# Transfers around a triangular solve moved from SyncE to GpSimd, the solve emitted later, and a norm's root moved to VectorE

## Chip, cores and metric

The kernel runs on one core of one Trainium2 chip. The metric is the device time of one execution in microseconds (us), and the median of several runs is compared. The engines are called by their names in the profile: PE (TensorE, matmuls; PEld is its weight loads), DVE (VectorE), ACT (ScalarE), POOL (GpSimd) and SP (SyncE). SP computes nothing here. It issues DMA transfers, and the row SPq shows its queue. Each engine works through its own queue in a fixed order.

## The reference

One decoder layer on 256 tokens with a model width of 2048: a norm, one input projection, two groups of heads side by side (an RWKV-7 recurrence with 16 heads of 64, and a latent attention with 8 heads), an output projection, a gated MLP with a short convolution, and a last norm. Cut to what matters here:

```python
def rwkv7_scan(r, w, k, v, a, b):
    def step(state, inp):
        r_t, w_t, k_t, v_t, a_t, b_t = inp
        sa = jnp.einsum('bhvk,bhk->bhv', state, a_t)
        state = (state * w_t[:, :, None, :]
                 + sa[..., None] * b_t[:, :, None, :]
                 + v_t[..., None] * k_t[:, :, None, :])
        return state, jnp.einsum('bhvk,bhk->bhv', state, r_t)
    ...

def rwkv7_mixer(...):
    ...
    y = rwkv7_scan(r, decay, k, v, -kk, kk * a)
    mu = jnp.mean(y, axis=-1, keepdims=True)
    var = jnp.mean(jnp.square(y - mu), axis=-1, keepdims=True)
    y = ((y - mu) * lax.rsqrt(var + GN_EPS)).reshape(bsz, s, c) * gn_w + gn_b
    bonus = jnp.sum(r * k * r_k, axis=-1, keepdims=True) * v
    return (y + bonus.reshape(bsz, s, c)) * g
```

The kernel doesn't run 256 steps. It cuts the sequence into four chunks of 64 tokens. Within a chunk the steps depend on each other through a unit triangular 64x64 matrix for each head, and the inverse of that matrix turns a chunk into a few matmuls.

## The kernel before

**Projections.** `in_tile(i)` (line 189) makes one of the 35 tiles of the input projection: 128 columns by 256 tokens, in one `mm` accumulator of PSUM. There are three such accumulators. A tile is made in two halves. For each, SP loads 512 KB of weights (`raw`, three buffers, line 127), ACT rounds them to fp32r (`hi`, line 133), DVE takes the rest (`lo`, line 134), and PE does eight matmuls with `hi` (line 163) and eight with `lo` (line 166). `hi` and `lo` have three buffers each. Tiles 17 to 24 are the value tiles, tiles 27 to 34 the latents of the attention.

**Eviction.** `shifted` (line 369) empties an accumulator: POOL clears one column of `h` (line 371), ACT copies one half of the accumulator (line 171), DVE adds the other half and scales (lines 172 and 173), ACT and DVE mix each token with the one before it (lines 374 and 375). The result is `sh`. After each pair of value tiles PE transposes them (line 612) and ACT copies them to `UV` (line 616).

**Deferred work.** `pend` holds pairs of a count and a function. `flush`, at the end of `in_tile`, calls the functions whose count is 0 and counts the others down. So a pair with count 0 is emitted after the next tile's matmuls, with count 1 after the next but one, and ahead of that tile's eviction.

**The solve and its transfers.**
- `gram` (line 511) multiplies keys and receptances of two pairs of heads on PE, and DVE masks the products into `G1` (line 529). At every second pair of tiles, 16 transfers of 16 KB (line 537, on SP) write the strict triangles of 32x32 blocks to `dL` in DRAM, two batches in all.
- `solve_load` (line 564) loads `dL` back as `Lp`, with one block per partition: 16 heads, 4 chunks and 2 diagonal blocks make 128. This is the factor.
- `solve` (line 568) inverts all the 128 blocks at once on DVE: one product with the key norms (line 575), then 31 steps of two products and sums (lines 579 and 581) on `Tq`, and a transposed copy `tp` (line 585). POOL clears `Tq` and `TT` ahead of it.
- The results go back through DRAM: `Tq` to `dT` (line 583), `tp` to `dU` (line 590), `dU` to `T11` (line 592) and `dT` to `TT` (line 596), the last two with a change of layout, all on SP.
- PE merges the blocks to 64x64 inverses (`pR`, line 625, and `pT`, line 638).

**Chunks.** `chunk(c)` (line 661) runs the recurrence: PE `px` from the state, DVE `XB`, PE `px` with `TT`, copies to `UV`, PE `pS` and `py`, DVE `ST` (the state). `group_norm(w)` (line 712) works on two chunks at a time; its root (line 723) is `rsqrt` (line 196), which is a first guess on the bits and three Newton steps. On POOL, the default, that is 14 instructions; on DVE, 11, since two steps are fused.

**Order.** A scheduler orders the instructions of each engine when the program is built, by a model of time and by the order in which the code emits them. `tc.issue_after(ins)` makes what is emitted in its block stand behind `ins` on that engine; it is an order, not a wait.

Of the kernel before, what the change touches and what calls it, by code (L numbers as in the profile page):

```python
# [9 lines left out]
F32 = mybir.dt.float32  # L10
# [4 lines left out]
ALU = mybir.AluOpType  # L15
AX = mybir.AxisListType

P = 128
# [7 lines left out]
GN_EPS = 64e-5  # L26
# [28 lines left out]
def hybrid_layer(ctx: ExitStack, tc: tile.TileContext, a: dict, out: bass.AP):  # L55
    nc = tc.nc
    V, S, PE = nc.vector, nc.scalar, nc.tensor
# [4 lines left out]
    dr = ctx.enter_context(tc.tile_pool(name="dr", bufs=1, space=bass.MemoryType.DRAM))  # L62
# [3 lines left out]
    def nm(s):  # L66
        uid[0] += 1
        return f"{s}{uid[0]}"
# [28 lines left out]
    def ch(n="ch"):  # L97
        return ps.tile([P, 512], F32, tag="ch", name=nm(n), bufs=NCH)
# [4 lines left out]
    def con(shape, n, dt=F32):  # L103
        return sb.tile(shape, dt, name=n, bufs=1)
# [10 lines left out]
    def vv(name, i, rows=slice(0, P)):  # L115
        return vec[rows, VOFF[name] + i:VOFF[name] + i + 1]
# [28 lines left out]
                                               h.bitcast(F32), ALU.mult, ALU.subtract).ins  # L145
        return raw

    last_w, last_lo, last_x = [None], [None], [None]
    pend = []


    def flush(every=False):
        now = [f for n, f in pend if n == 0 or every]
        pend[:] = [(n - 1, f) for n, f in pend if n > 0 and not every]
        for f in now:
            f()
# [32 lines left out]
    def in_tile(i, pf=mm):  # L189
        acc = pf()  # L190
        for h in range(2):
            prod_b(acc, piece(a["win"][i, h]), x_hl, h * 8, 8, h == 0, h == 1)
        flush()
        return acc
# [174 lines left out]
    def shifted(acc, i, rows=slice(0, P), dst=None):  # L369
        h = t1("h", 257)  # L370
        nc.gpsimd.memset(h[rows, 0:1], 0.0)
        joined(h[rows, 1:257], acc, rsB, rows)
        o = t1("sh") if dst is None else dst
        S.activation(o[rows], h[rows, 1:257], AF.Copy, scale=om_mu[rows, i:i + 1])
        V.scalar_tensor_tensor(o[rows], h[rows, 0:256], vv("mu", i, rows), o[rows], ALU.mult, ALU.add)
        return o


# [65 lines left out]
    for p in range(8):  # L444
        pp, g = p // 2, p % 2
# [23 lines left out]
    Mp = con([P, 32], "Mp")  # L469
# [21 lines left out]
    dL = dr.tile([P, 32, 32], F32, name="dL")  # L491
    dLv = dL.rearrange("(h b c p) i t -> b c i h p t", h=2, b=2, c=4)
    boP = ch("boP")
    bon = con([64, 64], "bon")
    for p in range(8):
        pp, g = p // 2, p % 2
        acc = in_tile(9 + p)
        if p == 0:
            pend.append((0, key_norms_p))
        r = shifted(acc, 9 + p)  # L500
        rc = r.rearrange("p (c t) -> p c t", t=64)
        V.tensor_tensor(AR[pp][:, g, :, 1, :], rc, AR[pp][:, g, :, 1, :], ALU.mult)
        pr = t1("pr")
        V.tensor_tensor(pr.rearrange("p (c t) -> p c t", c=4), kv_(pp, g), AR[pp][:, g, :, 1, :], ALU.mult)

        def bonus(p=p, pr=pr):
            for w in range(2):
                PE.matmul(boP[:, w * 16 + p * 2:w * 16 + p * 2 + 2], pr[:, w * P:(w + 1) * P], brk[:, p, :],
                          start=True, stop=True)

        def gram(p=p, pp=pp):
            hf = p // 4
            e0 = (pp % 2) * 2
            for c in range(4):
                if pp % 2 == 0:
                    G1[c].append(s4(n="G1").rearrange("p (e t) -> p e t", e=8))
            for w in range(2):
                pg = [ch("pg") for _ in range(2)]
                for r in range(2):
                    for gg in range(2):  # L520
                        o = (r * 2 + gg) * P
                        for h in range(2):
                            hs = slice(h * 64, h * 64 + 64)
                            PE.matmul(pg[h][:, o:o + P], BK[pp][hs, gg, w * 2 + r, :, :],  # L524
                                      AR[pp][hs, gg, w * 2 + r, :, :], start=o == 0, stop=True,
                                      skip_group_check=True)
                for h in range(2):
                    for r in range(2):
                        V.tensor_tensor(G1[w * 2 + r][hf][:, h * 4 + e0:h * 4 + e0 + 2, :],
                                        pg[h][:, r * T:(r + 1) * T].rearrange("p (q t) -> p q t", q=2),  # L530
                                        gmask.unsqueeze(1).broadcast_to([P, 2, P]), ALU.mult)
            if pp % 2 == 1:
                for c in range(4):
                    for b in range(2):
                        r0 = 64 + b * 32
                        for h in range(2):
                            nc.sync.dma_start(dLv[b, c, :, h, hf * 4:hf * 4 + 4, :],
                                              G1[c][hf][r0:r0 + 32, h * 4:h * 4 + 4, b * 32:(b + 1) * 32])
            for c in range(3):
                if pp == 0:  # L540
                    BKt.append(s4(n="BKt").rearrange("p (a t) -> p a t", a=8))
                pt = ch("pt")
                for gg in range(2):
                    PE.transpose(pt[:, gg * P:(gg + 1) * P],
                                 BK[pp][:, gg, c, :, :].rearrange("p s t -> p (s t)"), ident)
                S.copy(BKt[c][:, pp * 2:pp * 2 + 2, :], pt[:, 0:T].rearrange("p (a t) -> p a t", a=2))

        pend.append((0, bonus))
        if g == 1:
            pend.append((0, gram))  # L550
# [8 lines left out]
    TT = con([P, 32, 64], "TT")  # L559
    T11 = []  # L560

    Lps = []

    def solve_load():
        Lps.append(sv("Lp").rearrange("p (i t) -> p i t", i=32))
        nc.sync.dma_start(Lps[0], dL)

    def solve():
        Lp = Lps[0]
        Tq = sv("Tq").rearrange("p (s t) -> p s t", s=32)  # L570
        tm = t1("tm")
        nc.gpsimd.memset(Tq, 0.0)
        nc.gpsimd.memset(Tq.rearrange("p s t -> p (s t)")[:, 0:1024:33], 1.0)
        nc.gpsimd.memset(TT, 0.0)
        V.tensor_tensor(Lp, Lp, Mp.unsqueeze(1).broadcast_to([P, 32, 32]), ALU.mult)
        for i in range(31):
            n, m = i + 1, 31 - i
            tv = tm[:, 0:n * m].rearrange("p (s t) -> p s t", s=n)
            V.tensor_tensor(tv, Tq[:, 0:n, i:i + 1].broadcast_to([P, n, m]),
                            Lp[:, i:i + 1, i + 1:32].broadcast_to([P, n, m]), ALU.mult)  # L580
            V.tensor_tensor(Tq[:, 0:n, i + 1:32], Tq[:, 0:n, i + 1:32], tv, ALU.add)
        dT = dr.tile([P, 32, 32], F32, name="dT")
        nc.sync.dma_start(dT, Tq)
        tp = sv("tp").rearrange("p (s t) -> p s t", s=32)
        V.tensor_copy(tp, Tq.rearrange("p s t -> p t s"))
        dU = dr.tile([2, 32, 32, 32], F32, name="dU")
        for h in range(2):
            T11.append(sv("T11").rearrange("p (q s) -> p q s", q=32))
        for h in range(2):
            nc.sync.dma_start(dU[h], tp[h * 64:h * 64 + 32])  # L590
        for h in range(2):
            nc.sync.dma_start(T11[h][64:96], dU[h].rearrange("q s t -> s q t"))
        for h in range(2):
            for b in range(2):
                k0 = h * 64 + b * 32
                nc.sync.dma_start(TT[k0:k0 + 32, :, b * 32:(b + 1) * 32], dT[k0:k0 + 32].rearrange("q s t -> s q t"))

    pend.append((0, solve_load))
    pend.append((1, solve))


    UV = [s4(n="UV").rearrange("p (e t) -> p e t", e=8) for _ in range(4)]
# [2 lines left out]
    for pp in range(4):  # L605
        vt = []
        for g in range(2):
            vt.append(shifted(in_tile(17 + pp * 2 + g), 17 + pp * 2 + g))
        pt = ch("pv")
        for g in range(2):  # L610
            for w in range(2):
                PE.transpose(pt[:, (g * 2 + w) * P:(g * 2 + w + 1) * P], vt[g][:, w * P:(w + 1) * P], ident)
        ptv = pt.rearrange("p (g w t) -> p g w t", g=2, w=2)
        for w in range(2):
            for r in range(2):
                S.copy(UV[w * 2 + r][0:64, pp * 2:pp * 2 + 2, :], ptv[r * 64:r * 64 + 64, :, w, :])
# [95 lines left out]
    def group_norm(w):  # L712
        y = yt[w]
        y3 = y.rearrange("p (h v) -> p h v", h=16)
        mu = st("gmu", 16)
# [4 lines left out]
        S.activation(sq, y, AF.Square)  # L720
        va = st("gva", 16)
        V.tensor_reduce(va, sq.rearrange("p (h v) -> p h v", h=16), AX.X, ALU.add)
        rv = rsqrt(va, 1.0 / 64, GN_EPS, 16)
        V.tensor_tensor(y3, y3, rv.unsqueeze(2).broadcast_to([P, 16, 64]), ALU.mult)
        V.tensor_tensor(y, y, gnwb[0], ALU.mult)
        V.tensor_tensor(y, y, gnwb[1], ALU.add)
# [165 lines left out]
    for half in range(2):  # L892
# [3 lines left out]
        for c in range(4):  # L896
# [9 lines left out]
            if half == 1:  # L906
# [3 lines left out]
                for j in range(2):  # L910
                    pt = ch("pxT").rearrange("p (k t) -> p k t", k=2)
                    for k in range(2):
                        for tb in range(2):
                            o = (j * 2 + k) * P
# [34 lines left out]
    for blk, nf in enumerate((24, 20)):  # L949
# [33 lines left out]
        for c in range(4):  # L983
            accs = [mm() for _ in range(2)]
            for i in range(n - (4 if blk == 1 and c == 3 else 0)):
                prod_a(accs, piece(a["wdn"][c, f0 // 2 + i]), h_hi, h_lo, i * 2, 2, i == 0, i == n - 1)
                if blk == 1 and i == 2:
                    q = n - 4 + c
                    held.append((q, piece(a["wdn"][3, f0 // 2 + q], a8("wt"))))
            for tb in range(2):  # L990
# [7 lines left out]
                o = tb * 4 + c  # L998
# [88 lines left out]
```

## Time and profile before

| | |
|---|---|
| three runs, median (lowest to highest) | 1208.08 us (1207.26 to 1211.85) |
| profiled execution | 1207.02 us |
| its span, first to last instruction | 1205.2 us |
| mean granted PE clock | 0.987 of full speed |
| instructions | 18442 |

The time of an execution is 1.8 us longer than the span. In the profile, a row of a group gives line, engine, operation, output<-inputs, count, busy time and mean of one; a row of the timeline gives start, duration, and in brackets the idle time of the engine just before it with what ended it. A row of stages gives the busy time of each engine within that stretch, and PEclk the share of the full PE clock that was granted.

### The profile page before, as it was taken

How to read it: one execution, taken by the hardware profiler on the slowest of the kernel's cores; microseconds unless marked ns; L12 is line 12 of the kernel's file. 1: busy time of each engine (PE TensorE's matmuls, PEld its weight loads, DVE VectorE, ACT ScalarE, POOL GpSimd, SP SyncE). 2: the span in 40 equal slices, each digit the busy share in tenths (PEclk: the TensorE clock that was granted, in tenths of full speed). 3: DMA queues.
4: the chain of work that ended last, by engine and by line, in shares of the span. 5: the costliest groups of instructions: out<-in, count | busy, mean ns of one | idle time of the engine just before them, and what ended most of it. 6: DMA issues, size and time to landing. Idle time of an engine off the chain costs nothing.

```text
span 1205.2 us, 18442 instructions
## 1 busy us (share of the span) xinstructions
PE 1161.3 (96%) x6993; PEld 992.1 (82%) x6993; DVE 837.3 (69%) x1360; ACT 598.2 (50%) x939; POOL 58.3 (5%) x206
## 2 busy tenths in 40 slices
PE   7899988998799999999999999999999999999996
PEld 6788877887677888888888888888888888888885
DVE  7798759977887556777777776444577777775563
ACT  6784435533444455655555554333355555554451
POOL 1500100011110001000000000000000000000000
PEclk9999998998899999999999999999999999999998
DMA  8544454654133555555555555555655555566661
GB/s 329 177 151 153 144 141 145 204 151 145 54 126 120 191 176 175 194 192 192 192 193 192 193 191 181 193 194 190 204 193 193 192 190 190 190 218 209 209 221 76
DMA packets 71017, 215.82 MB, mean 179 GB/s; under 512 B 17616, under 2 KB 17872, under 8 KB 70928
## 3 DMA queue, kind: packets, MB, share of 16 engines
q1 hardware_dynamic: 69776, 211.84, 53.5%
q10 hardware_dynamic: 768, 2.05, 0.5%
q8 instruction: 55, 0.90, 0.3%
q0 software_dynamic: 384, 0.75, 0.3%
q14 instruction: 34, 0.28, 0.1%
HBM read 210.48 MB, written 3.41 MB: 177 GB/s over the span
## 4 chain that ended last, share of the span: by engine, by line
PE 88%; DVE 7%; POOL 2%; issue 1%; DMA 1%; ACT 0%; SPq 0%; ACTq 0%; DVEq 0%; POOLq 0%
PE mm L163 36%; PE mm L166 18%; PE mm L185 9%; PE mm L183 9%; PE mm L184 9%; DVE lo L134 1%; PE pg L524 1%; PE py L674 1%; PE px L674 1%; POOL sinR L292 0%; DMA raw<-in_win 0%; DMA Lp<-dL 0%; POOL cosR L288 0%; DVE tw L415 0%; PE pS L674 0%
## 5 line engine op out<-in xcount | busy, mean ns | idle before, releaser
L134 DVE TENSOR_TENSOR lo<-raw,hi 128x1024 fp32r<-128x1024 f32 x376 | 460.3, 1225 | 286.6 <-ACT hi L133 277.5
L133 ACT CAST hi<-raw 128x1024 fp32r<-128x1024 f32 x376 | 395.0, 1051 | 458.0 <-issue 250.2
L163 PE MATMUL mm<-z,hi 128*128 128x512 f32 x1408 | 351.3, 392 | 0.0
L163 PEld LDWEIGHTS mm<-z,hi 128*128 128x128 f32 x1408 | 251.9, 188 | 43.7
L166 PEld LDWEIGHTS mm<-z,lo 128*128 128x128 f32 x1408 | 188.3, 188 | 14.5
L166 PE MATMUL mm<-z,lo 128*128 128x256 f32 x1408 | 191.6, 278 | 0.0
L163 PE MATMUL mm<-x,hi 128*128 128x512 f32 x528 | 142.2, 406 | 20.0 <-DVE h L172 12.0
L184 PE MATMUL mm<-lo,hh 128*128 128x512 f32 x336 | 130.7, 389 | 0.0
L185 PE MATMUL mm<-hi,hl 128*128 128x512 f32 x336 | 130.7, 389 | 0.0
L163 PEld LDWEIGHTS mm<-x,hi 128*128 128x128 f32 x528 | 95.8, 193 | 37.5 <-ACT hi L133 8.0
L183 PE MATMUL mm<-hi,hh 128*128 128x512 f32 x336 | 119.7, 389 | 0.0
L166 PEld LDWEIGHTS mm<-x,lo 128*128 128x128 f32 x528 | 73.6, 191 | 7.0 <-issue 1.0
L166 PE MATMUL mm<-x,lo 128*128 128x256 f32 x528 | 78.9, 285 | 0.0
L185 PEld LDWEIGHTS mm<-hi,hl 128*128 128x128 f32 x336 | 63.1, 188 | 13.2
L184 PEld LDWEIGHTS mm<-lo,hh 128*128 128x128 f32 x336 | 63.1, 188 | 13.0
L183 PEld LDWEIGHTS mm<-hi,hh 128*128 128x128 f32 x336 | 63.1, 188 | 13.0
L184 PE MATMUL mm<-lo,yhi 128*128 128x512 f32 x128 | 51.1, 399 | 0.0
L185 PE MATMUL mm<-hi,ylo 128*128 128x512 f32 x128 | 50.5, 394 | 0.0
L183 PE MATMUL mm<-hi,yhi 128*128 128x512 f32 x128 | 49.6, 405 | 0.0
L961 POOL MEMSET gt<- 128x2 f32 x44 | 4.3, 100 | 575.9 <-DVE hl L973 572.8
L185 PEld LDWEIGHTS mm<-hi,ylo 128*128 128x128 f32 x128 | 24.1, 188 | 5.5 <-DVE ylo L746 0.4
L183 PEld LDWEIGHTS mm<-hi,yhi 128*128 128x128 f32 x128 | 23.9, 188 | 5.7 <-DVE kn L172 0.8
(290 smaller groups left out, 1124.2 us busy)
## 6 DMA issues: line engine op xcount, KB each, us to landing
raw<-in_wgu SPq DMA_DIRECT2D x176, 512.0 KB, 3.3
raw<-in_wdn SPq DMA_DIRECT2D x88, 512.0 KB, 4.1
raw<-in_win SPq DMA_DIRECT2D x70, 512.0 KB, 4.0
raw<-in_wout SPq DMA_DIRECT2D x32, 512.0 KB, 3.3
raw<-in_wuq SPq DMA_DIRECT2D x6, 512.0 KB, 4.2
xraw<-in_xT SPq DMA_DIRECT2D x4, 512.0 KB, 6.2
xt<-in_x SPq DMA_DIRECT2D x4, 512.0 KB, 6.6
raw<-in_wuv SPq DMA_DIRECT2D x4, 512.0 KB, 3.3
```

Of the source, the lines that this page charges most:

```text
L133: S.copy(hi, raw)
L134: last_lo[0] = V.tensor_tensor(lo, raw, hi.bitcast(F32), ALU.subtract).ins
L163: PE.matmul(acc, hi[:, j * P:(j + 1) * P], act(kt0 + j), start=first and j == 0, stop=False, skip_group_check=True)
L166: PE.matmul(acc[:, :T], lo[:, j * P:(j + 1) * P], act(kt0 + j)[:, 0, :], start=False, stop=last and j == n - 1, skip_group_check=True)
L183: PE.matmul(accs[tb], ah, wh, start=first and j == 0, stop=False)
L184: PE.matmul(accs[tb], ah, wl, start=False, stop=False)
L185: PE.matmul(accs[tb], al, wh, start=False, stop=last and j == n - 1)
L524: PE.matmul(pg[h][:, o:o + P], BK[pp][hs, gg, w * 2 + r, :, :], AR[pp][hs, gg, w * 2 + r, :, :], start=o == 0, stop=True, skip_group_check ...
L674: PE.matmul(dst[HS[h], a_ * 64:(a_ + 1) * 64], lhsT, rhs, start=n == 0 and a_ == 0, stop=True, skip_group_check=True)
L961: nc.gpsimd.memset(gt[:, 0:2], 0.0)
```

## The change

- The stores to `dL`, the load of `Lp`, and the transfers `dT`, `dU`, `T11` and `TT` are issued by POOL and no longer by SP.
- `dU` goes out ahead of `dT`, and the two `T11` transfers ahead of the four `TT` transfers, both by an explicit order on POOL.
- `solve()` is no longer in `pend`. It is emitted after the eviction of the third value tile (`pp == 1`, `g == 0`), and its first DVE product is ordered behind that eviction's last DVE operation, which `shifted` now keeps in `last_sh`.
- The root in `group_norm` is computed on DVE.

```diff
-    last_w, last_lo, last_x = [None], [None], [None]
+    last_w, last_lo, last_x, last_sh = [None], [None], [None], [None]
...
-        V.scalar_tensor_tensor(o[rows], h[rows, 0:256], vv("mu", i, rows), o[rows], ALU.mult, ALU.add)
+        last_sh[0] = V.scalar_tensor_tensor(o[rows], h[rows, 0:256], vv("mu", i, rows), o[rows],
+                                            ALU.mult, ALU.add).ins
...
-                            nc.sync.dma_start(dLv[b, c, :, h, hf * 4:hf * 4 + 4, :],
+                            nc.gpsimd.dma_start(dLv[b, c, :, h, hf * 4:hf * 4 + 4, :],
...
-        nc.sync.dma_start(Lps[0], dL)
+        nc.gpsimd.dma_start(Lps[0], dL)
...
-        V.tensor_tensor(Lp, Lp, Mp.unsqueeze(1).broadcast_to([P, 32, 32]), ALU.mult)
+        with tc.issue_after(last_sh[0]):
+            V.tensor_tensor(Lp, Lp, Mp.unsqueeze(1).broadcast_to([P, 32, 32]), ALU.mult)
...
-        dT = dr.tile([P, 32, 32], F32, name="dT")
-        nc.sync.dma_start(dT, Tq)
...
         for h in range(2):
-            nc.sync.dma_start(dU[h], tp[h * 64:h * 64 + 32])
+            du = nc.gpsimd.dma_start(dU[h], tp[h * 64:h * 64 + 32]).ins
+        with tc.issue_after(du):
+            nc.gpsimd.dma_start(dT, Tq)
         for h in range(2):
-            nc.sync.dma_start(T11[h][64:96], dU[h].rearrange("q s t -> s q t"))
-        for h in range(2):
-            for b in range(2):
-                k0 = h * 64 + b * 32
-                nc.sync.dma_start(TT[k0:k0 + 32, :, b * 32:(b + 1) * 32], dT[k0:k0 + 32].rearrange("q s t -> s q t"))
+            t11 = nc.gpsimd.dma_start(T11[h][64:96], dU[h].rearrange("q s t -> s q t")).ins
+        with tc.issue_after(t11):
+            for h in range(2):
+                for b in range(2):
+                    k0 = h * 64 + b * 32
+                    nc.gpsimd.dma_start(TT[k0:k0 + 32, :, b * 32:(b + 1) * 32],
+                                        dT[k0:k0 + 32].rearrange("q s t -> s q t"))
...
-    pend.append((1, solve))
...
             vt.append(shifted(in_tile(17 + pp * 2 + g), 17 + pp * 2 + g))
+            if pp == 1 and g == 0:
+                solve()
...
-        rv = rsqrt(va, 1.0 / 64, GN_EPS, 16)
+        rv = rsqrt(va, 1.0 / 64, GN_EPS, 16, V)
```

More of the change, by code (lines that the diff above doesn't have):

```diff
@@ L586, in solve @@
         dU = dr.tile([2, 32, 32, 32], F32, name="dU")
+        dT = dr.tile([P, 32, 32], F32, name="dT")
         for h in range(2):
```

## The prediction

> **What bounds the kernel now.** I read the page's busy times first, then the busy times cut by stage, then the timeline of the one stage in which TensorE (PE) stood still, then what PE waited for.
>
> ```profile
> span 1205.2 us, 18442 instructions
> PE 1161.3 (96%) x6993; PEld 992.1 (82%) x6993; DVE 837.3 (69%) x1360; ACT 598.2 (50%) x939; POOL 58.3 (5%) x206
> ```
> ```profile
> core 0: us, PE busy (x) PEld busy (x) DVE busy (x) ACT busy (x) POOL busy (x), PEclk, DMA share, GB/s
> 165.00:177.00 12.00, 11.96 (x85) 10.33 (x85) 6.03 (x11) 4.14 (x7) 0.00 (x0) 1.00 0.37 79
> 177.00:190.00 13.00, 5.78 (x21) 4.83 (x22) 8.75 (x25) 3.31 (x7) 0.10 (x1) 0.74 0.43 159
> 190.00:235.00 45.00, 45.00 (x268) 39.73 (x267) 42.75 (x91) 28.60 (x50) 0.29 (x3) 1.00 0.62 177
> 235.00:262.00 27.00, 27.00 (x398) 23.58 (x398) 19.43 (x30) 8.08 (x13) 3.71 (x14) 1.00 0.72 194
> 262.00:340.00 78.00, 65.78 (x825) 54.14 (x824) 58.47 (x105) 31.15 (x62) 10.20 (x32) 0.91 0.32 104
> 340.00:470.00 130.00, 127.70 (x615) 103.15 (x614) 88.50 (x142) 62.76 (x118) 6.14 (x14) 1.00 0.47 158
> ```
> PE is the bound: 44 of 1205 us without a matmul. Two stages that the change touches hold 19 of these: 7.2 us around the load of the factor (13.00 - 5.78) and 12.2 us in the chunk recurrences (78.00 - 65.78). From 190 to 262 us, where the solve runs and its transfers go out, PE is never idle: time saved there is worth nothing by itself.
>
> ```profile
> 166.56 9.06 SPq L537 DMA_DIRECT2D dL<-G  x16
> 171.55 0.76 DVE L529 TENSOR_TENSOR G<-pg,cst 128x256 f32<-128x256 f32 x2 [0.83 <-PE pg L524]
> 176.83 0.38 ACT L171 COPY h<-mm 128x256 f32<-128x256 f32 x1
> 176.94 5.12 DMA Lp<-dL
> 182.09 1.23 DVE L575 TENSOR_TENSOR Lp<-Lp,Mp 128x1024 f32<-128x1024 f32 x1 [3.81 <-DMA Lp<-dL]
> 183.75 0.42 DVE L172 TENSOR_TENSOR h<-mm,h 128x256 f32<-128x256 f32 x1
> 184.22 3.78 PE L163 MATMUL mm<-x,hi 128*128 128x512 f32 x8 [7.26 <-DVE h L172]
> 187.80 1.40 PE L166 MATMUL mm<-x,lo 128*128 128x256 f32 x8
> 192.27 2.00 PE L163 MATMUL mm<-x,hi 128*128 128x512 f32 x8
> 191.36 1.07 PE L166 MATMUL mm<-x,lo 128*128 128x256 f32 x7
> ```
> Read it from the bottom up. PE could not start a tile because all three mm accumulators were full; the first came free with the eviction at 183.75. That eviction belongs to the second value tile and stood in VectorE's (DVE's) queue behind L575, the solve's first operation, which waited 3.81 us for the factor. The factor was loaded at 176.94, behind 16 small stores on SP, of which the last half needed the masking at 171.55. After the gap PE also ran cold: eight matmuls in 3.78 us for 2.00, and the next eight in 1.40 for about 1.1. **The stall costs 7.2 + 1.8 + 0.3 = 9.3 us.**
>
> **The change, part by part.** *The solve's place.* It was emitted ahead of the second value tile's eviction; now it stands behind the third's, on DVE by an explicit order. So the second and third tile are evicted when PE is done with them, two accumulators are free, and PE can fill two more tiles (about 5.5 us each, two halves of eight L163 and eight L166) whatever DVE waits for in the solve. That takes away the 9.3 us as they stand. What is late next is the split of the weights (L134), also on DVE: behind a waiting L575 stand the lo halves, and PE has two halves in hand, 2 x 2.75 = 5.5 us.
>
> *The factor by POOL.* 32 stores, one load, dU, dT, T11 and TT go from SP to GpSimd (POOL). Nothing in the trace shows POOL issuing a strided transfer; it shows four kinds of plain ones, and how SP fared:
>
> ```profile
> L432 POOL DMA_DIRECT2D kraw<-kraw x1 | 0.6, 607 | 1.1 <-DVE kraw L173 1.1
> L434 POOL DMA_DIRECT2D ksw<-kraw x4 | 2.0, 514 | 0.0
> L805 POOL DMA_DIRECT2D qs<-qr x4 | 2.0, 504 | 0.3 <-issue 0.3
> L247 POOL DMA_DIRECT2D rp<-in_pos x1 | 0.8, 763 | 0.3 <-issue 0.3
> ```
> ```profile
> dL<-G SPq DMA_DIRECT2D x32, 16.0 KB, 1.6
> qs<-qr POOLq DMA_DIRECT2D x4, 128.0 KB, 3.7
> ksw<-kraw POOLq DMA_DIRECT2D x4, 32.0 KB, 1.8
> ```
> An issue took 514 ns for 32 rows, 607 for 64, 763 for 128: about 0.43 us + 2.6 ns a row (estimate, a line through three rows). A dL store has 128 runs of 32 numbers: 0.76 us by the line, 0.50 if runs cost nothing, 2.0 if all of an issue went with its rows (16 ns each). Seven stores wait for the masking that ends at 172.3: 7 x 0.76 = 5.3, so 177.6; landing 1.7 more; the load 0.76 and some 4.5 to land: **the factor arrives near 185, 3 us later than now** (183 to 194 between the ends). If DVE waits from 178.3, where it began to wait before, to 185, that is 6.7 us plus one split of 1.23, against 5.5 in hand: I take 2 us of new PE idle, 0 at best, 9 at worst. SP, for its part, is rid of 9.06 us of issuing, but PE lost only 0.04 us in that stretch (11.96 of 12.00): worth 0.
>
> The Trainium skill, "DMA: Bandwidth & Descriptors", sections "SWDGE vs HWDGE vs iDMA" and "Latency and other measured facts", speaks against this part: GpSimd computes its descriptors in software where SP has hardware for it, and the first byte comes after about 1 us against 0.6. By that page each of the four dependent steps (dL, Lp, dU, TT) would come 0.4 us later, 1.6 us in all (estimate). The landings above (1.8 us from POOL, 1.6 from SP) lean that way, for other sizes (32 and 16 KB).
>
> *Behind POOL's transfers* now stand the one-column memsets of h, which shifted() needs, the clearing of UV and Tq, and the norms' roots.
>
> ```profile
> 242.10 0.18 POOL L201 TENSOR_SCALAR rm<-ssm 128x2 f32<-128x2 f32 x1 [44.18 <-DVE ssm L774]
> 246.92 0.17 DVE L776 TENSOR_SCALAR rr<-ry 128x2 f32<-128x2 f32 x1 [1.79 <-POOL ry L216]
> ```
> POOL will issue 16 x 0.76 = 12 us twice, held up by the maskings. POOL is idle 95% of the span and memsets can go ahead by a tile; I take 0.5 us lost, 0 to 3. The first latent's root ran at 242 and moves some 9 us up with PE, before dU goes out; if it fell behind the T11 transfers, DVE would wait at L776.
>
> *The solve's results.*
>
> ```profile
> 234.74 1.14 DVE L585 COPY tp<-Tq 128x1024 f32<-128x1024 f32 x1
> 235.91 1.04 SPq L590 DMA_DIRECT2D dU<-tp  x2
> 240.37 1.37 SPq L592 DMA_DIRECT2D T<-dU  x2
> 241.79 2.11 SPq L596 DMA_DIRECT2D TT<-dT  x3
> 245.50 0.31 PE L625 MATMUL pR<-T,G 32*32 32x32 f32 x4
> 251.50 3.93 PE L638 MATMUL pT<-TT,RT 32*32 32x32 f32 x128
> ```
> Two T11 and four TT transfers have 1024 runs each: 0.43 + 1024 x 2.6 ns = 3.1 us by the line (0.5 as qs for the same bytes, 16 if all went with rows). Six take 18.6 us on POOL, where SP took 0.32 + 1.37 + 2.11 = 3.8. With the factor's 3 us the merge (L638) could start some 18 us later than now. What hides it: PE comes 9 us earlier to this place, and the queries' and values' projections (14 pieces of 2 to 3 us) need no solve. The scheduler writes that order, and I count the delay at 0; without the cover it costs up to 18.
>
> *The root on DVE.*
>
> ```profile
> 310.01 2.45 DVE L729 TENSOR_TENSOR gsq<-UV,bon 64x1024 f32<-64x1024 f32 x2
> 310.07 1.23 POOL L201 TENSOR_SCALAR rm<-gva 128x16 f32<-128x16 f32 x1 [23.32 <-DVE gva L722]
> 316.29 1.23 DVE L724 TENSOR_TENSOR yt<-yt,ry 128x1024 f32<-128x1024 f32 x1 [2.07 <-POOL ry L216]
> 321.22 0.96 PE L166 MATMUL mm<-cl,lo 128*128 128x256 f32 x4 [2.09 <-DVE lo L134]
> 363.25 1.23 DVE L724 TENSOR_TENSOR yt<-yt,ry 128x1024 f32<-128x1024 f32 x1 [1.93 <-POOL ry L216]
> L257 DVE TENSOR_SCALAR rp<-rp 128x64 f32<-128x64 f32 x3 | 0.6, 196 | 0.1
> ```
> POOL's 14 instructions (6.2 us, 310.07 to 316.25) become 11 on DVE at 0.17 to 0.20 us (L776's 128x2 and L257's 128x64 bracket 128x16): 2.0 us. DVE waits 2.07 and 1.93 us less and works 2.0 more each time; the chain gets 4 us shorter, DVE no freer. I take 0.5 us gained, 0 to 4.
>
> **Sum:** -9.3 + 2 + 0.5 - 0.5 = -7.3 us. The span and its launch took 1207.0 us in the profiled execution, so 1199.7; the median of the three runs stands 1.1 us above it (1208.1): **1200.8**.
>
> **The rivals.** *(a) The stall only moves.* The factor comes at 185 or later, DVE stands at L575 and the lo splits with it. For it: PE needs a split every 2.75 us and DVE is in order. Against: 5.5 us in hand. Worst term 9 for 2: 1207.5, no change. *(b) POOL's issue times hold up the merge.* PE's order is fixed before the run; if it counts on SP's spacing, PE stands at the pR and pT matmuls. With half of the 18 us covered, 9 us later than before: 1217. It decides from about 2.8 us a transposing transfer (6 x 2.8 - 3.8 = 13, half covered, = 6.5 us) on; at 0.5 us it vanishes. For: 1024 runs against at most 128 seen. Against: the fillers. A harsher form: the Trainium skill, "SBUF — State Buffer", section "A bandwidth-pool intuition that's wrong", says that such a transfer grew from 0.62 to 3.1 us beside a DVE copy, since GpSimd could not write its descriptors. By it six transfers would take 18.6 us, and the time would be the same 1217; it has 0.02 of the chance of (b). The qs transfers above ran beside DVE products at 504 ns, so the trace shows none of it, but no copy either. *(c) The chunk stage gains too.* Earlier weights on SP and a root that is 4 us sooner fill 7 of the 12.2 idle us: 1193. *(d) The transfers do nothing* and only the place counts: the forecast without its 2: 1199.
>
> **Chances.** Forecast with (d) 0.50 (own range 1195 to 1205), (a) 0.17, (b) 0.20, (c) 0.13. Within 0.5% is about what a measurement of this kernel can tell from no change: 1202.0 to 1214.1. Faster: 0.42 of the 0.50, and (c): 0.55. Same: 0.08 + 0.17 + 0.02 of (b) = 0.27. Slower: 0.18. Range 1190 to 1217: the upper end takes in half of (b), the lower end (c).
>
> **What would show it.** Right: PE near 13 of 13 us in the stage after the factor's stores; the evictions of the second and third value tiles within 2 us of their last matmul; L575 behind the third L375. Wrong by (a): an L134 or an mm matmul released late, with a DVE wait for Lp of over 7 us. Wrong by (b): POOL rows for T11 and TT above 2.8 us each, and PE waiting at L625 or L638. Root: no POOL rows for gva, eleven short DVE rows ahead of L724. The prediction falls if the scheduler puts the later tiles' evictions behind the whole solve: then the accumulators fill up as before.

## The result and the profile after

The kernel after takes 1216.08 us (median of 5 runs, 1215.16 to 1216.83), the kernel before 1208.33 us beside it (5 runs). The ratio is 1.0058, 95% interval [1.0042, 1.0074]: slower by 0.6%, where faster was forecast. The span of the profiled execution is 1215.1 us (before 1205.2), the mean granted clock 0.981 (before 0.987).

The head of the page of the kernel after, then its busy times by the stages that the prediction used (columns as there):

```profile
span 1215.1 us, 18447 instructions
...
PE 1168.3 (96%) x6993; PEld 999.7 (82%) x6993; DVE 841.5 (69%) x1382; ACT 598.7 (49%) x939; POOL 71.8 (6%) x220
```
```profile
165.00:177.00 12.00, 12.00 (x85) 10.19 (x85) 8.25 (x15) 4.46 (x8) 8.45 (x16) 1.00 0.51 147
177.00:190.00 13.00, 12.58 (x78) 11.04 (x76) 5.15 (x5) 6.89 (x11) 1.96 (x7) 1.00 0.66 210
190.00:235.00 45.00, 41.88 (x236) 36.79 (x237) 42.30 (x94) 26.94 (x48) 0.20 (x2) 0.96 0.55 164
235.00:262.00 27.00, 22.41 (x246) 19.70 (x245) 18.16 (x35) 7.25 (x9) 10.14 (x23) 0.92 0.76 212
262.00:340.00 78.00, 65.56 (x924) 55.97 (x922) 57.79 (x111) 26.84 (x55) 5.83 (x18) 0.83 0.23 76
```

PE works 12.58 of 13.00 us around the factor's load, where it worked 5.78. But from 190 to 262, where it was never idle before, it now stands 7.71 us (3.12 + 4.59), and from 262 to 340 the granted clock is 0.83 instead of 0.91. PE is busy 7.0 us *longer* in all (1168.3 against 1161.3) for the same matmuls. The mean granted clocks account for that (an estimate: 1161.3 x 0.987 / 0.981 = 1168.4). The timeline of the kernel after shows the places (line numbers are up to 6 higher than before):

```profile
176.66 0.55 POOL L538 DMA_DIRECT2D dL<-G  x1 [0.55 <-DMA dL<-G]
...
180.91 0.56 POOL L567 DMA_DIRECT2D Lp<-dL  x1 [3.70 <-DMA dL<-G]
...
189.75 1.22 DVE L134 TENSOR_TENSOR lo<-raw,hi 128x1024 fp32r<-128x1024 f32 x1 [1.50 <-ACT hi L133]
190.90 1.22 DVE L577 TENSOR_TENSOR Lp<-Lp,Mp 128x1024 f32<-128x1024 f32 x1
...
192.55 0.42 DVE L172 TENSOR_TENSOR h<-mm,h 128x256 f32<-128x256 f32 x1
...
193.12 1.19 PE L163 MATMUL mm<-x,hi 128*128 128x512 f32 x2 [3.54 <-DVE tm L581]
...
244.64 1.12 DVE L585 COPY tp<-Tq 128x1024 f32<-128x1024 f32 x1
246.06 1.07 POOL L591 DMA_DIRECT2D dU<-tp  x2 [2.06 <-DVE tp L585]
...
252.03 1.11 PE L166 MATMUL mm<-x,lo 128*128 128x256 f32 x8
...
253.40 3.11 POOL L600 DMA_DIRECT2D TT<-dT  x4 [1.63 <-DMA dT<-Tq]
...
255.86 0.31 PE L631 MATMUL pR<-T,G 32*32 32x32 f32 x4 [1.34 <-DMA T<-dU]
...
261.64 3.59 PE L644 MATMUL pT<-TT,RT 32*32 32x32 f32 x64 [1.98 <-DMA TT<-dT]
...
265.16 1.12 PE L680 MATMUL px<-UV,G 128*64 128x64 f32 x16
```

The first chunk products and the last input projection of the kernel before:

```profile
255.37 0.69 PE L674 MATMUL px<-UV,G 128*64 128x64 f32 x16
...
262.47 1.07 PE L166 MATMUL mm<-x,lo 128*128 128x256 f32 x8
```

The factor is issued at 180.91 and lands 4.6 us later, near 185.5. The solve's first product doesn't wait for it: it runs at 190.90. Six splits (L134) stand on DVE between the third value tile's eviction (173.94) and this product, where e1 below has three, and all but one of them waited for ACT. PE's 3.54 us at 193.12 are again a full accumulator. The row names L581, but what frees an accumulator is the eviction, here L172 of the fourth value tile, which stands on DVE behind L577 and runs at 192.55. So a part of the old stall came back; e1 has none of it. The solve begins 8.8 us later than before, its copy (L585) comes 9.9 us later (244.64 against 234.74), the merge 10.4 (pR 255.86 against 245.50), and the end 9.9. PE by then is 10 us *ahead* with the input projections (their last matmul ends at 253.1, before at 263.5), runs out of work ahead of the merge, and does the merge and the first chunk cold: the first 16 chunk products take 1.12 us where they took 0.69.

### The profile page after: what moved, and what is told of

Same layout as the page of the kernel before. It is cut to its first block, busy times and chain, and to the rows that moved or that the text cites. A ratio compares the mean times of both kernels' runs of the same rounds, so it can differ in the third digit from the quotient of the medians.

```text
span 1215.1 us, 18447 instructions
## 1 busy us (share of the span) xinstructions
PE 1168.3 (96%) x6993; PEld 999.7 (82%) x6993; DVE 841.5 (69%) x1382; ACT 598.7 (49%) x939; POOL 71.8 (6%) x220
## 4 chain that ended last, share of the span: by engine, by line
PE 88%; DVE 5%; DMA 3%; POOL 2%; issue 1%; ACT 1%; ACTq 0%; SPq 0%; DVEq 0%; POOLq 0%
PE mm L163 35%; PE mm L166 18%; PE mm L183 9%; PE mm L184 9%; PE mm L185 9%; PE pg L525 1%; DVE lo L134 1%; DMA xt<-in_x 1%; PE px L680 1%; DMA TT<-dT 1%; PE pT L644 1%; PE py L680 1%; DMA dT<-Tq 0%; POOL sinR L290 0%; DVE tw L416 0%
## 5 line engine op out<-in xcount | busy, mean ns | idle before, releaser
L134 DVE TENSOR_TENSOR lo<-raw,hi 128x1024 fp32r<-128x1024 f32 x376 | 460.5, 1225 | 287.1 <-ACT hi L133 280.2
```

Of the source, the lines that this page charges most:

```text
L134: last_lo[0] = V.tensor_tensor(lo, raw, hi.bitcast(F32), ALU.subtract).ins
```

## The experiments

The question after the traces: is it the place, the transfers or the root? And why does a stall that goes bring nothing? Ratios are against the kernel before, run on the same chip. "Copy" is the start of the solve's copy `tp`, "px" the first chunk product, both from the profiled execution.

| | ratio [95%] | copy | px | span | span - px |
|---|---|---|---|---|---|
| before | 1 | 234.7 | 255.4 | 1205.2 | 949.8 |
| after | 1.0058 [1.0042, 1.0074] | 244.6 | 265.2 | 1215.1 | 949.9 |
| e1 place | 1.0016 [1.0005, 1.0027] | 242.0 | 260.8 | 1210.2 | 949.4 |
| e2 transfers | 1.0074 [1.0051, 1.0097] | 242.1 | 269.7 | 1221.4 | 951.7 |
| e3 root | 0.9995 [0.9984, 1.0006] | 235.5 | 256.1 | 1205.2 | 949.1 |
| e4 second tile | 1.0026 [1.0013, 1.0039] | 243.7 | 265.0 | 1213.6 | 948.6 |
| e7 relief, before | 0.9957 [0.9942, 0.9973] | 232.4 | 253.6 | 1200.0 | 946.4 |
| e8 relief, place | 0.9992 [0.9983, 1.0000] | 237.9 | 259.1 | 1206.1 | 947.0 |
| e9 warm, place | 0.9990 [0.9979, 1.0001] | 241.0 | 261.5 | 1205.0 | 943.5 |
| e10 results on POOL | 1.0059 [1.0047, 1.0071] | 241.1 | 264.7 | 1213.2 | 948.5 |
| e11 inputs on POOL | 1.0040 [1.0027, 1.0053] | 242.4 | 261.6 | 1210.6 | 949.0 |
| e12 warm, relief, place | 1.0012 [1.0003, 1.0020] | 237.1 | 258.2 | 1207.5 | 949.3 |
| e13 hold, place | 0.9967 [0.9955, 0.9979] | 234.8 | 255.7 | 1204.5 | 948.8 |
| e14 hold, after | 1.0065 [1.0050, 1.0079] | 238.9 | 269.3 | 1216.8 | 947.5 |
| e15 splits on POOL, before | 1.0069 [1.0055, 1.0083] | 233.5 | 256.3 | 1217.1 | 960.8 |
| e16 splits on POOL, place | 1.0077 [1.0056, 1.0098] | 238.7 | 260.4 | 1216.6 | 956.2 |
| e17 hold, relief, place | 0.9947 [0.9933, 0.9961] | 233.6 | 253.2 | 1202.3 | 949.1 |
| e18 hold, after, root | 1.0070 [1.0057, 1.0082] | 239.4 | 267.4 | 1216.5 | 949.1 |

The last column is the finding in short: **the end goes with the first chunk product.** Apart from e9, e15 and e16, it lies between 946 and 952 us ahead of the end, however PE stood before it. These are single profiled executions, and the link isn't tested by itself.

**The change in three parts.** e1 has the place alone (transfers on SP in their old order, root on POOL), e2 the issue from POOL alone, e3 the root alone, e4 is e1 with the solve one tile earlier.

```diff
 # e1, on before
+        with tc.issue_after(last_sh[0]):
             V.tensor_tensor(Lp, Lp, Mp.unsqueeze(1)...
-    pend.append((1, solve))
...
+            if pp == 1 and g == 0:      # e4: pp == 0 and g == 1
+                solve()
 # e2, on before: nc.sync.dma_start -> nc.gpsimd.dma_start for dL, Lp, dU, dT, T11, TT
 # e3, on before
+        rv = rsqrt(va, 1.0 / 64, GN_EPS, 16, V)
```

> Only the solve's new place (emitted behind the third value tile, first product behind its last shift); all transfers stay on SP, the root stays on POOL. Theory A (the solve was late because the POOL transfers made the scheduler put three more weight splits ahead of its first product): three splits fewer stand ahead of it, it starts near 183 instead of 190.9, its copy ends near 237, the merge starts near 247, the stall at the factor load goes, and the time is 1199 to 1206. Theory B (the place itself is at fault: the tensor engine outruns the merge whoever issues): start and end as in the kernel after, 1212 to 1217.

> Only the issue from GpSimd (dL stores, Lp load, dU, dT, T11, TT, with the new order of dU and dT); the solve stays in its old place, the root on POOL. Theory A: the first product keeps its old place in DVE's queue and waits for Lp until about 185.5 (before: 182.1), the landings of T11 and TT cost another 3, so the merge starts 4 to 7 us later than before and the time is 1212 to 1215. Theory B: the transfers are nearly free, 1208 to 1210.

> Only the root of the second norm on DVE. Theories A and B: no more than 1 us either way, 1207 to 1209.5. Theory C (the 2 us that the kernel after loses at the last norm are the root's, whose six small instructions stand behind other work of DVE): 1210 to 1211.

> As e1_place, but the solve is emitted behind the second value tile. It tells whether one tile more or less ahead of the solve matters once the transfers are on SP. Theory A: within 3 us of e1_place, both under 1207. Theory B: between the kernel before and e1_place, 1209 to 1214, since less of the tensor engine's work runs ahead of the merge.

Measured: +0.16%, +0.74%, -0.05% (no change) and +0.26%. Theory A was half right: with SP the first product does run at 183.29, but the time isn't shorter, and at 1211.9 us it stands next to theory B's. e4 is B's in size and against it in sense: B had it faster, and it is no faster than e1. e2 is worse than either had it. The stages of e1, and the stretch from its first product to the end of its copy:

```profile
177.00:190.00 13.00, 13.00 (x81) 11.61 (x80) 9.03 (x19) 7.91 (x14) 0.20 (x2) 1.00 0.73 247
190.00:235.00 45.00, 45.00 (x266) 39.72 (x266) 42.48 (x89) 26.89 (x47) 0.71 (x4) 1.00 0.59 187
235.00:262.00 27.00, 24.40 (x353) 22.03 (x352) 16.02 (x31) 5.86 (x8) 3.37 (x12) 0.82 0.66 175
262.00:340.00 78.00, 63.83 (x799) 52.37 (x800) 57.74 (x104) 28.40 (x57) 10.79 (x32) 0.82 0.26 84
183.29:243.10 59.81, 59.61 (x353) 52.59 (x352) 55.33 (x121) 34.89 (x58) 4.18 (x16) 1.00 0.58 181
```

The same stretch of the kernel before:

```profile
182.09:235.88 53.79, 51.66 (x291) 45.27 (x292) 51.15 (x115) 32.55 (x58) 0.39 (x4) 0.94 0.54 156
```

And the splits of the weights on DVE within these two stretches, before and e1 (count, busy time, mean ns):

```profile
L134 DVE TENSOR_TENSOR lo<-raw,hi 128x1024 fp32r<-128x1024 f32 x17 | 20.8, 1223 | 1.5 <-ACT hi L133 1.1
```
```profile
L134 DVE TENSOR_TENSOR lo<-raw,hi 128x1024 fp32r<-128x1024 f32 x21 | 25.7, 1224 | 1.6 <-ACT hi L133 1.3
```

The stall is gone for good (13.00 of 13.00). The solve, however, takes 59.8 us instead of 53.8, and *DVE* is busy 51.15 of 53.79 us in it before, 55.33 of 59.81 in e1. PE, let ahead by the new place, needs the splits of more tiles; four more of them (4.9 us by the rows above) stand among the solve's steps (20 up to the copy instead of 16; both counts above, and those in the expectations below, have one more, which begins as the copy ends). Of the 6.0 us by which the stretch grows, 4.2 are DVE's work. What PE wins, DVE pays out of the solve. At the merge PE then stands:

```profile
248.29 0.62 PE L166 MATMUL mm<-cl,lo 128*128 128x256 f32 x4
250.37 0.31 PE L628 MATMUL pR<-T,G 32*32 32x32 f32 x4 [1.45 <-DMA T<-dU]
251.30 0.88 PE L628 MATMUL pR<-T,G 32*32 32x32 f32 x44 [0.62 <-DMA T<-dU]
```

One piece that needs no solve (`mm<-cl`) stands ahead of pR in PE's order, not fourteen. In e2 the old stall got longer, as rival (a) of the prediction has it; here is its timeline:

```profile
186.94 1.22 DVE L576 TENSOR_TENSOR Lp<-Lp,Mp 128x1024 f32<-128x1024 f32 x1 [6.25 <-DMA Lp<-dL]
...
189.07 3.78 PE L163 MATMUL mm<-x,hi 128*128 128x512 f32 x8 [9.70 <-DVE h L172]
```

**Is DVE the bound?** e5 and e6 leave every second step of the solve out, with the old and the new place; e7 and e8 take one product a tile off DVE.

```diff
 # e5 (on before), e6 (on e1)
-        for i in range(31):
+        for i in range(0, 31, 2):
 # e7 (on before), e8 (on e1); late is set for the last six value tiles and the latents
-        V.tensor_tensor(dst, dst, scale[rows], ALU.mult)
+        (nc.gpsimd if late[0] else V).tensor_tensor(dst, dst, scale[rows], ALU.mult)
```

> The kernel before with every second step of the solve left out (16 of 31 are done; the factors are not the reference's). Theory D (the tensor engine's projections ahead of the merge are a fixed stock, and the merge is set by the solve's chain on DVE, so a stall removed ahead of the solve comes back at the merge): the chain is some 25 us shorter, the merge comes with pieces of the projections left, which fill the chunk stage; 1195 to 1203. Theory E (the solve's place costs by itself, whatever the chain's length): the time is nearly that of before, 1205 to 1209.

> e1_place with every second step of the solve left out in the same way. Theory D: now the 7 us of the stall at the factor load are real, 6 to 9 us under e5_short_before. Theory E: 1 to 3 us above e5_short_before, as with the whole solve.

> The kernel before with the scaling by rsB (one 128x256 product of 0.42 us a tile) given to GpSimd for the last six value tiles and the eight latent tiles. Theory D (DVE's queue sets the solve's end): 14 products or 5.9 us leave DVE's queue, about 10 of them inside the solve; the merge comes 3 to 5 us earlier, 1204 to 1207. Theory G (the latency of each solve step sets its end, and DVE has room): no gain, 1208 to 1211, since each eviction takes longer on GpSimd.

> e1_place with the same products given to GpSimd. Theory D: 4 to 7 us under e1_place, 1204 to 1208, and it gains more from this than the kernel before does, because its solve shares DVE with more tiles. Theory G: as e1_place, 1211 to 1213.

e5: 0.9908 [0.9890, 0.9926]; e6: 0.9912 [0.9895, 0.9929], its first chunk product at 232.5. Both theories missed on the pair: the two can't be told apart. A chain that is shorter by half gives 11 us in either place. In e6 the first chunk product comes 28 us earlier than in e1 and the time only 12.6: span - px grows to 964.6, since PE still has projections to do when the chunks run. Whether e5 is the same isn't shown. e7 is as theory D says: 0.43% faster, the copy 2.3 us earlier; e8 is 0.24% under e1, about 3 us of the 4 to 7 forecast.

**The cold clock, and the two sides of the transfers.** e9 and e12 give PE useless work ahead of the merge; e10 issues only the results from POOL, e11 only the inputs, both on e1.

```diff
 # e9 (on e1), e12 (on e8), ahead of the first pR product
+        for _ in range(16 if qh == 0 else 0):
+            PE.matmul(pr_[:, 0:P], ident, tps[0]...[:, 0:P], start=True, stop=True, ...)
```

> e1_place with 16 useless 128x128 products of tp (about 2.4 us of the tensor engine's time), written into the merge's first PSUM tile before its real products, so that the tensor engine doesn't stand still ahead of the merge. In e1_place it stands 2.07 us there and the granted clock is then 0.50 from 252 to 276. Theory H (that half clock through the merge and the first chunk is what gives the stall's gain back): the merge and the first chunk run at 1.00, 1204 to 1208, although work is added. Rival (the merge's length is set by DVE and the landings, not by the clock): 1211 to 1214.

> e1_place with only the solve's results (dU, dT, T11, TT, in the order of the change) issued by GpSimd; dL's stores and Lp stay on SP. The first product keeps e1_place's place in DVE's queue, so the solve starts near 183.3 as there. If the 5 us between e1_place and the kernel after come from the inputs' side (three splits more ahead of the first product): 1212 to 1214. If they come from the results' longer landings (6.5 and 7.3 us against 3.5 and 4.0): 1215 to 1218.

> e1_place with only dL's stores and Lp's load issued by GpSimd; the results stay on SP. The first product stands three splits further back in DVE's queue. If that is what costs: it starts near 190.9 as in the kernel after and the time is 1214 to 1217; if the results' landings cost instead: 1211 to 1213.

> e8_relief_place with the same 16 useless products. Theory H: the clock holds at 1.00 through the merge, 4 to 6 us under e8_relief_place, 1202 to 1205, level with e7_relief_before. Rival: as e8_relief_place, 1207 to 1210.

e9 came out at 0.9990, e1 at 1.0016; but its first chunk product isn't earlier (261.5 against 260.8), and the clock fell all the same, only a little later (0.77 from 252 to 256, where e1 has 0.52; its stages are shown at the end). The gain lies behind 300 us: from there to 345 PE works 40.97 us, in e1 37.75. The edit changed the planned order; which change of it helped is open. So theory H isn't shown, and e12, slower than e8, speaks against it: there PE is warm until 256, the first chunk product comes 0.9 us earlier, and the time is not shorter.

e10 and e11 split the transfers: against e1 the results cost 0.43% (5.2 us), the inputs 0.24% (2.9 us). Each came out inside the range that was expected if its side is the costly one, so both sides cost. They don't add up: 8.1 us together, while the kernel after, which has both, stands 5.1 us above e1, as e10 alone does. In e10 the cost is seen at the merge: PE waits 3.91 and 2.60 us for `T` at pR, where e1 waits 1.45 and 0.62. e11 is also the clearest sign for DVE. Its solve starts 6.9 us later than e1's (190.2 against 183.3) and its copy only 0.4 later (242.4 against 242.0): much the same stands ahead of the copy in DVE's queue. Three of its splits now come before the first product instead of behind (six behind the third value tile's eviction, e1 three), and one falls behind the copy. Its stretch from first product to copy:

```profile
190.20:243.50 53.30, 51.06 (x299) 45.03 (x300) 50.02 (x116) 30.28 (x52) 4.00 (x16) 1.00 0.57 174
```

**The test.** e13 removes no work. It only holds the splits of the last two latent tiles back until the copy is through; e14 does so in the kernel after. e15 and e16 move every second split of a late tile to GpSimd, on e7 and e8.

```diff
 # e13 (on e1), e14 (on after)
+        with tc.issue_after(held_by[0]) if held_by[0] is not None else nullcontext():
             last_lo[0] = V.tensor_tensor(lo, raw, hi.bitcast(F32), ALU.subtract).ins
...
+            held_by[0] = tpc[0] if x * 4 + j >= 6 else None     # tpc: the copy tp
             acc = in_tile(27 + x * 4 + j)
 # e15, e16
+        if late[0] and nth[0] % 2:
+            nc.gpsimd.tensor_tensor(lo, raw, hi.bitcast(F32), ALU.subtract)
```

> e1_place with the weight splits of the last two latent tiles held behind the solve's copy in DVE's queue; nothing is left out. Theory D (DVE's queue between the first product and the copy is the bound): 16 splits instead of 21 stand in it, so the copy comes 5 to 6 us earlier (near 237), the merge near 246, with one to two tiles left to fill it; 1203 to 1207. Rival (the tensor engine's tiles pace the solve): the copy stays near 242, 1210 to 1214.

> The kernel after, whole, with the same splits held back: 13 instead of 18 stand between the first product and the copy. Theory D: the copy comes 4 to 6 us earlier (near 239.5 instead of 244.6) and the time is 1209 to 1213. Rival: as the kernel after, 1215 to 1217.

> e7_relief_before with, besides, the second weight split of each of the last fourteen input tiles given to GpSimd (estimated at four times the 0.80 to 0.89 us of its 128x256 product, 3.2 to 3.6 us each, under a tile's 5.6 us on the tensor engine). Theory D: some ten splits of 1.22 us leave DVE's queue ahead of the copy, which comes near 223 to 226, and the merge near 235; the chunk stage gets projections to fill it; 1196 to 1201. Rival (GpSimd's longer splits starve the tensor engine): 1204 to 1212.

> The same on e1_place. Theory D: with room on DVE the tiles that run ahead no longer delay the solve, and the removed stall counts at last: 2 to 7 us under e15_pool_split_before. Rival (the place brings nothing even then, because the projections' work only moves): within 1.5 us of e15_pool_split_before or above it.

e13 does what theory D says, and its stages show it:

```profile
177.00:190.00 13.00, 13.00 (x79) 11.50 (x78) 9.21 (x19) 7.68 (x14) 0.20 (x2) 1.00 0.81 249
190.00:235.00 45.00, 45.00 (x268) 39.85 (x267) 42.15 (x95) 27.25 (x47) 1.68 (x9) 1.00 0.57 174
235.00:262.00 27.00, 25.33 (x387) 21.65 (x388) 18.54 (x27) 5.51 (x9) 4.53 (x6) 0.87 0.72 196
...
183.10:235.90 52.80, 52.80 (x312) 46.67 (x311) 49.81 (x112) 31.91 (x54) 2.61 (x11) 1.00 0.58 172
```

The length of the stretch goes with the number of splits in it: 16 in the kernel before (53.8 us), after (54.9), e11 (53.3) and e13 (52.8), 20 in e1 (59.8). So e13's copy is at 234.8 instead of 242.0 and its first chunk product at 255.7 instead of 260.8, and the kernel is 0.49% faster than e1. It is also 0.33% faster than the kernel before, though its first chunk product stands as there and the profiled spans differ by 0.7 us only; where that comes from isn't shown. The hold was not run in the old place, so how much of the 0.33% belongs to the new place stays open too. In e14, with 13 splits, the copy comes 5.7 us earlier too (238.9), but the time doesn't fall: the first chunk product is at 269.3, and 1218.55 us lies above what either theory had. Its timeline names a wait that the prediction feared, GpSimd's queue:

```profile
238.95 1.17 DVE L588 COPY tp<-Tq 128x1024 f32<-128x1024 f32 x1
...
240.03 3.49 DVE L136 TENSOR_TENSOR lo<-raw,hi 128x1024 fp32r<-128x1024 f32 x3
240.27 1.06 POOL L218 TENSOR_SCALAR rt<-rt 128x2 f32<-128x2 f32 x1
...
243.53 1.08 POOL L594 DMA_DIRECT2D dU<-tp  x2
...
249.26 0.82 POOL L598 DMA_DIRECT2D T<-dU  x1 [3.89 <-DMA dU<-tp]
250.11 0.23 POOL L218 TENSOR_SCALAR rt<-rt 128x2 f32<-128x2 f32 x1
...
252.12 1.22 PE L228 MATMUL rsb<-dg,ones 128*128 128x128 f32 x4 [6.69 <-DVE dg L227]
```

e15 and e16 were slower than either theory had them, 1218.35 and 1219.73 us, and e16 is no faster than e15. Their first chunk products are in the place of e7 and e8 to within 3 us; the loss lies behind them (span - px 960.8 and 956.2). In e15 PE works only 42.22 of 53.00 us from 182 to 235, where it worked 50.78 before, so projections are left for later. So moving the splits away was tried and did not help; what it did to DVE is in the last section.

In e14 the first latent's root stands on POOL between the transfers, and PE waits for it. e18 takes it off POOL; e17 joins the two edits that helped.

```diff
 # e18, on e14
-        V.tensor_scalar(rr, rsqrt(m, 1.0 / 512, EPS, 2), post, None, ALU.mult)
+        V.tensor_scalar(rr, rsqrt(m, 1.0 / 512, EPS, 2, V), post, None, ALU.mult)
```

> e13_hold_place with the fourteen products by rsB on GpSimd (e8's edit). Theory D: DVE loses another five to six products between the first product and the copy, 1 to 3 us under e13_hold_place, 1203.5 to 1205.5. Rival (the two edits free the same time, and what remains is set by the merge and the chunk stage): 1205.5 to 1208.

> e14_hold_after with the roots of the two latents on DVE instead of GpSimd. If GpSimd's queue is what took e14's gain (the root behind T11's wait for dU, and dU itself behind root operations of about 1 us each while DVE copies and splits): dU is issued near 240 instead of 243.5, the 6.7 us wait at rsb goes, the merge starts near 252 to 254 instead of 259.7, and the time is 1209 to 1213. Rival (the hold itself starves the tensor engine): 1216 to 1219 as in e14.

e18 is no faster than e14 (1.0070 against 1.0065). dU does go out at 240.83 and the 6.69 us wait is gone, but PE waits 5.00 us at the next tile's accumulator instead. Its eviction (250.69) stands on DVE behind a split whose ACT step waited 8.03 us for weights. `T` and `TT` are there in time: PE waits for neither at pR (260.49) nor at pT (263.96). What makes the merge late is the projections ahead of it in PE's order, held up and then run at a lower clock (0.56 granted from 250 to 255; eight matmuls take 3.75 us at 251.25, the same eight 2.42 at 256.50). e13 has such a late split as well (ACT waits 7.84 us), but the eviction (240.65) stands ahead of the split (244.31) there. That difference is in the traces and was not tested, so why the hold helps with SP's transfers and not with POOL's stays open. e17 is the fastest kernel that does the whole solve: 1203.05 us, a little under its forecast, ratio 0.9947 [0.9933, 0.9961]. It can't be told apart from e7 (0.9957), which is the kernel before with 14 products moved and nothing else.

## Why the prediction was wrong, step by step

- **The step that failed** is the reading "From 190 to 262 us ... PE is never idle: time saved there is worth nothing by itself", and with it the terms "takes away the 9.3 us as they stand" and "I count the delay at 0". The row that it was read from has DVE busy 42.75 of 45.00 us. The merge waits for the solve, and the solve for its turn on DVE. Against the delay counted at 0, the copy came 7.3 us later in e1 and 9.9 in the kernel after, and the merge 4.9 and 10.4. A stall of PE ahead of it costs nothing as long as PE catches up before the merge; removed, it comes back there (e1), and as cold clock besides. Shortening DVE's queue ahead of the copy brings the time back (e13: 4 splits less, -0.49% against e1). That the place then gains anything by itself isn't shown: with the relief it costs (e8 0.9992, e7 0.9957), and with hold and relief it can't be told from e7 (e17 0.9947).
- *The cover.* "14 pieces need no solve" is true of the data, not of PE's order: one stood ahead of pR.
- *The factor near 185* was right (185.5), the issue of a dL store smaller than taken (0.55 us for 0.76). The term of +2 for DVE's wait measured +2.9 (e11 against e1), by another way: no wait for Lp at all, but a first product that the scheduler had put three splits further back.
- *The transposing transfers* were wrong by a factor of four in their issue (0.80 and 0.78 us for 3.1), so rival (b) fell by its cause; yet PE stood just where (b) has it, at pR and pT, and the time came out 0.9 us from its 1217, by another cause than (b) gave. The price lies in the landing, which the sum had left at SP's values. The transfers of the kernel after (KB each, median us from issue to landing):

```profile
dL<-G POOLq DMA_DIRECT2D x32, 16.0 KB, 2.6
Lp<-dL POOLq DMA_DIRECT2D x1, 512.0 KB, 4.6
...
TT<-dT POOLq DMA_DIRECT2D x4, 128.0 KB, 7.3
dU<-tp POOLq DMA_DIRECT2D x2, 128.0 KB, 3.2
T<-dU POOLq DMA_DIRECT2D x2, 128.0 KB, 6.5
```

  From SP it was, in this order, 1.6, 5.1, 4.0, 4.4 and 3.5 us. The harsher form by the Trainium skill, "SBUF — State Buffer", section "A bandwidth-pool intuition that's wrong", isn't seen in the issues: no transposing transfer took POOL over 0.83 us. The landings of these transfers did grow by about 3 us, and no run separates what DVE has in that from the wait behind the transfer issued just ahead. The 0.4 us a step that the prediction worked out from the Trainium skill's "DMA: Bandwidth & Descriptors", section "Latency and other measured facts", is too little for dL, T11 and TT (1.0, 3.0 and 3.3) and has the wrong sign for Lp and dU (-0.5 and -1.2).
- *The root* was forecast to shorten its chain by 4 us. From the end of gva's sum to the product that uses the root it took 6.3 us before (309.98 to 316.29) and 6.9 in e3 (310.79 to 317.69): each of its steps takes 0.17 us, but they stand between other instructions of DVE. Nothing gained, nothing lost.
- *What was to show it*: the evictions of the second and third value tile did come at once, L577 did stand behind the third L375, and PE did reach 12.58 of 13. The signs of "right" came true while the time went the other way; they all lay ahead of the merge. Half of (a)'s sign came too: a tile's first matmul was released 3.54 us late, but there was no wait of DVE for Lp. The sign that would have told was the time of the copy.
- *Small slips in the rivals' sums*: by the prediction's own terms (a) is 1200.8 + 7 = 1207.8 and not 1207.5, and (c) 1200.8 - 7 = 1193.8 and not 1193. Nothing hangs on it.

The parts sum to 0.16 - 0.05 + 0.74 = 0.85%, the whole is 0.58%. The difference lies within the intervals of the three ratios, and so does that between the whole and e2. That the new place is worth something with POOL's transfers, since it spares e2's longer stall, is therefore not shown; with SP's it costs.

## What to carry to other kernels

Ahead of a serial stage that waits for a chain on one engine, price a change by when that chain ends, not by the idle time of the busiest engine: look which engine is near 95% busy within the chain, and what else stands in its queue. Letting one engine run ahead isn't free when it draws support work (splits, evictions) from the engine that the chain needs; hold that work back behind the chain, or give it away. Neither is safe by itself: the hold helped in one kernel and not in another (e13, e14), and splits given to GpSimd cost more than they freed (e15, e16).

## What was not expected of the hardware

GpSimd's work beside DVE slows both. In e15 the solve's steps, 337 ns each before, took these times beside nine splits on GpSimd (2.47 us on average, six of them within the solve) and its other products, by its groups on DVE from 165 to 245:

```profile
L587 DVE TENSOR_TENSOR Tq<-Tq,tm 128x31 f32<-128x31 f32 (+15 forms) x31 | 19.8, 637 | 0.8
L585 DVE TENSOR_TENSOR tm<-Tq,Lp 128x31 f32<-128x31 f32 (+15 forms) x31 | 16.9, 546 | 0.9
```

That is 15.7 us more, and it ate what DVE had won: eleven splits fewer stand on it between the first product and the copy (5 instead of 16, 13.4 us). The other way round, e14's roots of 128x2 took 1.06 us instead of 0.23 while DVE split (240.27 above). The Trainium skill, "SBUF — State Buffer", section "SBUF: two separate sides", says that the two engines share a pair of ports as an exclusive lock; both rows agree with that.

A PE that is busy with 32x32 products can still lose its clock. e9's stages from 244 on:

```profile
244.00:248.00 4.00, 4.00 (x34) 3.82 (x33) 1.49 (x2) 0.00 (x0) 0.00 (x0) 1.00 1.01 304
248.00:252.00 4.00, 4.00 (x38) 3.24 (x39) 1.23 (x1) 1.05 (x1) 0.00 (x0) 1.00 1.31 163
252.00:256.00 4.00, 4.00 (x159) 3.76 (x155) 2.76 (x4) 0.00 (x0) 0.00 (x0) 0.77 0.65 239
256.00:260.00 4.00, 3.50 (x76) 3.37 (x74) 1.37 (x2) 0.00 (x0) 0.00 (x0) 0.50 0.02 4
```

PE shows no idle time up to 256, and the granted clock falls to 0.77 and 0.50. In the kernel before the same merge ran at 1.00, with projections between its products.
